# Second parts of the split of two blocks of FFN rows: made on VectorE instead of GpSimd

## The chip, the cores and the metric

One core of one Trainium2 chip runs the kernel. The metric is the device time of one execution in microseconds. The engines are named as the profile names them: PE is TensorE, DVE is VectorE, ACT is ScalarE, POOL is GpSimd, SP is the queue that issues most transfers.

## The reference, cut to what matters

One layer of a decoder for 512 prompt rows and 32 sample rows of width 1024: a mixer, cross-attention to a memory, and a gated feed-forward network (FFN) with a short convolution. The change lies where cross-attention ends and the FFN begins:

```python
x = x + rms_norm(mem_attend(rms_norm(x, g_mem_pre), mk, mv, w_mq, w_mo), g_mem_post)
f, conv_new = conv_ffn(rms_norm(x, g_ffn_pre), conv_buf, w_up, w_dw, b_dw, w_down)
x = x + rms_norm(f, g_ffn_post)
```

`rms_norm` divides each row by the root of its mean square and multiplies by a gain. `conv_ffn` first computes `u = h @ w_up`, with 5504 output columns.

## The kernel before

**Split products.** A float32 operand of a large product is kept as two parts in the format fp32r: a first part, the operand cast to fp32r, and a second part, the operand minus the first. A product is made of three matmuls: first by first, first by second, second by first. `split` makes both parts: the first always on ACT, the second on DVE, or on another engine if one is passed in. Weights are split in the same way after they arrive (tile `wst` into tile `wslot`, 128x1024 each).

**The boundary.** The rows lie in five blocks: blocks 0 to 3 with 128 prompt rows each, block 4 with the 32 sample rows. The last projection of cross-attention (tile `oT` times `w_mo`) goes through its second 512 output columns block by block, in the order 4, 0, 1, 2, 3 (`proj_add`, `second`). For each block `ev1` makes a sum of squares on ACT (`sqj`), a product with the gain on DVE (`y`, L1128), the sum `ssy` on DVE (L1129), the power -1/2 of it on POOL (`rs`, L304), and two additions into the residual rows `xb` on DVE (L1134). `rows_of` then makes the mean square of the new rows on ACT (`sqx`, L309), its power -1/2 on POOL, and a copy `rsd` on DVE, and puts the block on a list.

**Transposed rows.** `norm_turn` takes a block from that list. It transposes its 1024 columns on PE in two quads of four 128x128 tiles each (L328, into the PSUM tile `tp`), multiplies a quad by the gain on DVE (`ht`, L330), and splits it into the tiles of `fT` (first part on ACT, L146, second part L147). In the instruction order below `fT_6086` and `fT_6098` are the first parts of quads 0 and 1, and `fT_6087` and `fT_6099` the second parts. The tuple `pool` says for each quad whether its second part is made on POOL (`True`) or on DVE (`False`). The factor of each row isn't multiplied into `fT`; `spread` broadcasts it with a small matmul over the partitions (tile `rsb` in PSUM, one matmul for each block) and DVE copies it to SBUF (`rsb`, line 1565). The PSUM tiles `tp` and `rsb` share three buffers.

**The first FFN products.** The first four tiles of `u` are computed in two halves of rows (`half_first` in `gemmB`, L465): for columns 0 to 255 of `fT` (blocks 0 and 1) all four tiles, 24 matmuls each, and then for columns 256 to 543 (blocks 2, 3 and 4). Blocks 2 and 3 are transposed between the tiles of the first half (`POS`). All later tiles (L477) take both halves together.

**The order.** A scheduler decides at build time, from its own estimate of times, in which order each engine gets its instructions; each engine then keeps that order. So a change of one instruction's engine can move others.

```python
def split(hi, lo, src, eng=None):
    nc.scalar.copy(out=hi, in_=src)
    (eng or nc.vector).tensor_tensor(out=lo, in0=src, in1=f32(hi), op=SUB)
```

Of the kernel before, what the change touches and what calls it, by code (L numbers as in the profile page):

```python
# [77 lines left out]
def kernel(ctx: ExitStack, tc: tile.TileContext, I, O):  # L78
# [8 lines left out]
    ACTROWS, POOLQ = True, (True, True)  # L87
# [17 lines left out]
    def N(name, w=1024):  # L105
        return npool.tile([P, 1032], F32, name=name, tag="N")[:, :w]

    def T2(shape, name, dt=F32):
        return t2p.tile(list(shape), dt, name=name, tag="T2")

    def Z(name):
        return zp.tile([P, 512], F32, name=name, tag="Z")
# [36 lines left out]
    def rows(b):  # L149
        return (b * P, P) if b < 4 else (SEQ, NS)  # L150
# [147 lines left out]
    def rstd(ss, n, w, dim, name="rs"):  # L298

        r = small(w, name)  # L300
        if dim is not None:
            nc.gpsimd.tensor_scalar(out=r[:n], in0=ss, scalar1=1.0 / dim, scalar2=EPS, op0=MUL, op1=ADD)
            ss = r[:n]
        GTT(out=r[:n], in0=ss, in1=mhalf[:n, :w], op=ALU.pow)  # L304
        return r[:n]

    def sumsq(x, n, junk, name="ssq"):
        ss = small(1, name)
        ACT(out=junk, in_=x, func=AF.Square, accum_out=ss[:n])  # L309
        return ss[:n]  # L310

    def norm_rows(x, n, act=False):
        h = N("hN")[:n]
        rs = rstd(sumsq(x, n, h), n, 1, DM)
        if act:
            nc.scalar.mul(out=h, in_=x, mul=rs)
        else:
            VTS(out=h, in0=x, scalar1=rs, scalar2=None, op0=MUL)
        return h

    def norm_turn(h, n, gname, xt, c0, pool=(True, False)):

        tmps = []
        for q in range(2):
            ps = at("tp")
            pv = v2(ps, P)[:, :, :n]
            for j in range(4):
                tr(pv[:, j, :], h[:, (4 * q + j) * P:(4 * q + j + 1) * P], ident[:n, :n])  # L328
            tmp = T2([P, 4, n], "ht")
            VTT(out=tmp, in0=pv, in1=gcol(gname, 4 * q, 4 * q + 4).unsqueeze(2).broadcast_to([P, 4, n]), op=MUL)  # L330
            put(xt, q, 0, 4, c0, n, tmp, nc.gpsimd if pool[q] else None)
            tmps.append(tmp)
        return tmps
# [15 lines left out]
    class Fill:  # L349
# [8 lines left out]
        def run(self, amount=1e9):  # L358
            while amount > 0 and self.q:
                try:  # L360
                    amount -= next(self.q[0])
                except StopIteration:
                    self.q.pop(0)
# [25 lines left out]
    def sample_sum(ps, dst):  # L389
        for e in range(2):  # L390
            c = slice(256 * e, 256 * e + 256)
            nc.scalar.copy(out=dst[:, c], in_=ps[NS * e:NS * e + NS, :256])
            VTT(out=dst[:, c], in0=ps[64 + NS * e:64 + NS * e + NS, :256], in1=dst[:, c], op=ADD)
# [260 lines left out]
    for c0, c1 in HALF:  # L654
        n = c1 - c0
# [433 lines left out]
    def gbc(name):  # L1089
        g = cst.tile([P, 1028], F32, name="gb", tag="gb")  # L1090
        dma(out=g[:, :DM], in_=I[name][0].partition_broadcast(P))
        return g[:, :DM]

    def proj_add(xt, gname, src, gname2, dst, order=None, scale=None):

        g = gbc(gname)
        y0, s0, xb, pend, ready, target = {}, {}, {}, [], [], []

        def ssq(b, y, nm):
            n = rows(b)[1]  # L1100
            ss = sm.tile([P, 1], F32, name=nm, tag=nm, bufs=6)
            j = Z("sqj")
            ACT(out=j[:n], in_=y, func=AF.Square, scale=DM ** -0.5, accum_out=ss[:n])
            return ss[:n]

        def ev0(b, ps):
            n = rows(b)[1]
            z = y0[b] = T2([P, 512], "y0")[:n]
            if b == 4:
                sample_sum(ps, z)  # L1110
                ps = z
            s0[b] = ssq(b, ps, "ssy0")
            VTT(out=z, in0=ps, in1=g[:n, :512], op=MUL)

        def before(b):
            for c in [4, 0, 1, 2, 3] if scale else [b]:
                if c not in xb:
                    xb[c] = N("xb")[:rows(c)[1]]
                    dma(out=xb[c], in_=src(c))

        def ev1(b, ps):
            c0, n = rows(b)
            z = T2([P, 512], "y1")[:n]
            if b == 4:
                sample_sum(ps, z)
                ps = z
            ss = ssq(b, ps, "ssy1")
            VTT(out=z, in0=ps, in1=g[:n, 512:], op=MUL)  # L1128
            STT(out=ss, in0=s0[b], scalar=EPS, in1=ss, op0=ADD, op1=ADD)  # L1129
            rs = rstd(ss, n, 1, None)  # L1130
            x = xb[b]
            for i, z in enumerate((y0[b], z)):
                c = slice(512 * i, 512 * i + 512)
                STT(out=x[:, c], in0=z, scalar=rs, in1=x[:, c], op0=MUL, op1=ADD)  # L1134
            dma(out=dst[c0:c0 + n, :], in_=x)
            ready.append((x, n, c0))
            while len(ready) > LR:
                rows_of(*ready.pop(0))

        def rows_of(x, n, c0):  # L1140
            if scale is None:
                pend.append((norm_rows(x, n, ACTROWS), n, gname2, target[0], c0, POOLQ))
                return
            pend.append((x, n, gname2, target[0], c0, POOLQ))
            rs = sm.tile([P, 1], F32, name="rsd", tag="rsd", bufs=5)
            VCP(out=rs[:n], in_=rstd(sumsq(x, n, Z("sqx").bitcast(BF16)[:n]), n, 1, DM))
            scale[1].append((rs[:n], c0, n))

        def mid():
            if len(pend) > LP:  # L1150
                norm_turn(*pend.pop(0))

        def second(xt2):
            target.append(xt2)
            run(gemmA(xt, 8, [4, 0, 1, 2, 3], ev1, block_major=True, before=before, mid=mid, midk=1 if scale else MIDK))
            while ready:
                rows_of(*ready.pop(0))
            while len(pend) > 2:
                norm_turn(*pend.pop(0))
            return pend  # L1160
        return gemmA(xt, 8, order or allb, ev0, block_major=order is not None, halves=True), second
# [157 lines left out]
    pend = second(hqT)  # L1319
# [250 lines left out]
    pend = second(fT)  # L1570
# [307 lines left out]
```

## Time and profile before

| What | Value |
|---|---|
| time, median of 3 runs | 960.0 us (959.2 to 962.14) |
| profiled execution: its time, its span | 957.37 us, 955.6 us |
| PE busy in the span | 933.3 us, 98% |
| DVE busy | 600.3 us, 63% |
| ACT busy | 387.7 us, 41% |
| POOL busy | 196.4 us, 21% |
| mean granted clock of PE | 0.994 of full speed |

The span runs from the first to the last instruction of the profiled execution. Busy shares are means over stages with different limits. The boundary between cross-attention and FFN lies between 541 and 576 us of the span. Below, an instruction's row gives its start, its duration, and in brackets how long the engine sat idle ahead of it and what ended that.

### The profile page before, as it was taken

The page shows a single profiled execution, that of the slowest core. Times are in us where ns is not written, and L with a number is a line of the kernel's source. Part 1 is how long each engine was busy: PE and PEld are TensorE (multiplying, and loading weights), DVE is VectorE, ACT ScalarE, POOL GpSimd, SP SyncE. Part 2 cuts the span into 40 slices and gives each one's busy share as a digit, 9 for nine tenths or more (in the row PEclk, how much of TensorE's full clock was granted, in tenths as well). Part 3 has the DMA queues.
Part 4 walks back from the last instruction along what each step waited for, and adds up shares of the span by engine and source line. Part 5 has one row for each costly group of instructions (what it writes and reads, how often), then busy time and mean ns, then how long its engine had stood idle before and what let it go on. Part 6 is the DMA issues. An engine that isn't in the chain of part 4 may idle for free. (4 is left out here: it accounts for less than half of the span.)

```text
span 955.6 us, 17087 instructions
## 1 busy us (share of the span) xinstructions
PE 933.3 (98%) x6619; PEld 810.2 (85%) x6619; DVE 600.3 (63%) x1129; ACT 387.7 (41%) x750; POOL 196.4 (21%) x383
## 2 busy tenths in 40 slices
PE   8999999999999999999999999999999999999995
PEld 5899787889766778998767799989988997999974
DVE  6745145565886448635654769727758676676767
ACT  5655134344676357635544523332212222222232
POOL 6610000115432216300000454001110110110114
PEclk9999999999999999999999999999999999999998
DMA  8950023344825539946954743063053313512023
GB/s 296 296 178 1 1 88 136 88 131 137 275 82 171 173 100 346 289 137 188 344 195 115 206 133 88 4 177 89 4 144 82 119 26 81 162 48 89 24 92 116
DMA packets 120674, 130.27 MB, mean 136 GB/s; under 512 B 8568, under 2 KB 86233, under 8 KB 120593
## 3 DMA queue, kind: packets, MB, share of 16 engines
q1 hardware_dynamic: 114408, 125.69, 42.3%
q10 hardware_dynamic: 6184, 3.48, 1.2%
q8 instruction: 52, 0.85, 0.4%
q14 instruction: 30, 0.24, 0.1%
HBM read 112.22 MB, written 16.93 MB: 135 GB/s over the span
## 5 line engine op out<-in xcount | busy, mean ns | idle before, releaser
L146 ACT CAST wslot<-wst 128x1024 fp32r<-128x1024 f32 x125 | 130.8, 1050 | 261.3 <-issue 73.5
L477 PE MATMUL mm<-fT,wslot 128*128 128x256 f32 x1872 | 235.9, 288 | 0.0
L477 PEld LDWEIGHTS mm<-fT,wslot 128*128 128x128 f32 x1872 | 234.4, 188 | 1.8 <-issue 0.8
L147 DVE TENSOR_TENSOR wslot<-wst,wslot 128x1024 fp32r<-128x1024 f32 x125 | 154.4, 1238 | 91.8 <-ACT wslot L146 91.4
L1689 PE MATMUL mm<-wslot,act 128*128 128x512 f32 (+1 forms) x180 | 70.2, 391 | 0.0
L1690 PE MATMUL mm<-wslot,act 128*128 128x512 f32 (+1 forms) x180 | 70.0, 392 | 0.0
L1688 PE MATMUL mm<-wslot,act 128*128 128x512 f32 (+1 forms) x180 | 69.3, 387 | 0.0
L1596 POOL COPY cvo<-u 128x2 f32<-128x2 f32 x43 | 11.0, 256 | 204.7 <-DVE u L1594 194.6
L407 PE MATMUL mm<-wslot,hT 128*128 128x512 f32 x128 | 51.6, 403 | 0.0
L477 PE MATMUL mm<-hT,wslot 128*128 128x256 f32 (+1 forms) x384 | 51.0, 289 | 0.0
L409 PE MATMUL mm<-wslot,hT 128*128 128x512 f32 x128 | 51.0, 400 | 0.0
L408 PE MATMUL mm<-wslot,hT 128*128 128x512 f32 x128 | 50.7, 396 | 0.0
L1591 DVE TENSOR_TENSOR u<-mm,rsb 128x256 f32<-128x256 f32 x43 | 18.2, 424 | 51.0 <-PE mm L477 50.0
L477 PEld LDWEIGHTS mm<-hT,wslot 128*128 128x128 f32 x384 | 49.2, 188 | 0.5 <-issue 0.2
L1688 PEld LDWEIGHTS mm<-wslot,act 128*128 128x128 f32 x180 | 34.3, 191 | 8.0 <-issue 0.4
L1690 PEld LDWEIGHTS mm<-wslot,act 128*128 128x128 f32 x180 | 33.8, 188 | 7.2 <-issue 0.4
L1689 PEld LDWEIGHTS mm<-wslot,act 128*128 128x128 f32 x180 | 33.8, 188 | 7.2
L1608 ACT ACTIVATE c<-c 128x560 f32<-128x560 f32 x21 | 14.1, 672 | 56.5 <-DVE c L1602 56.5
L1602 DVE SCALAR_TENSOR_TENSOR c<-u,cvT,c 128x560 f32<-128x560 f32 x43 | 34.3, 798 | 0.9
L1601 DVE SCALAR_TENSOR_TENSOR c<-u,cvT,c 128x560 f32<-128x560 f32 x43 | 34.1, 793 | 0.2
L1701 DVE TENSOR_TENSOR yp<-mm,yp 128x512 f32<-128x512 f32 (+1 forms) x41 | 27.2, 674 | 5.1 <-PE mm L1690 5.0
L409 PEld LDWEIGHTS mm<-wslot,hT 128*128 128x128 f32 x128 | 24.1, 188 | 5.1
(474 smaller groups left out, 1863.8 us busy)
## 6 DMA issues: line engine op xcount, KB each, us to landing
wst<-in_w_up_dram SPq DMA_DIRECT2D x42, 512.0 KB
wst<-in_w_in_dram SPq DMA_DIRECT2D x28, 512.0 KB
wst<-in_w_down_dram SPq DMA_DIRECT2D x20, 512.0 KB
wst<-in_cache_mem_k_dram SPq DMA_DIRECT2D x16, 512.0 KB
wst<-in_w_mk_dram SPq DMA_DIRECT2D x8, 512.0 KB
xb<-in_x_prompt_dram SPq DMA_DIRECT2D x8, 512.0 KB
wst<-in_cache_dk_dram SPq DMA_DIRECT2D x16, 256.0 KB
wst<-in_cache_dv_dram SPq DMA_DIRECT2D x16, 256.0 KB
```

The costliest lines, as they stand in the source:

```text
L146: nc.scalar.copy(out=hi, in_=src)
L147: (eng or nc.vector).tensor_tensor(out=lo, in0=src, in1=f32(hi), op=SUB)
L407: mm(ps[b], lhsT=xt.hi(k, c0, c0 + n), rhs=s[:, 0, kk, :], start=(k == 0), stop=False)
L408: mm(ps[b], lhsT=xt.hi(k, c0, c0 + n), rhs=s[:, 1, kk, :], start=False, stop=False)
L409: return mm(ps[b], lhsT=xt.lo(k, c0, c0 + n), rhs=s[:, 0, kk, :], start=False, stop=(k == nk - 1))
L477: mm(ps[i], lhsT=s[:, l, k, :], rhs=x(k, c0, c1), start=(k == 0 and j == 0), stop=(k == 7 and j == 2))
L1601: STT(out=c, in0=u[:, 1:EXT - 1], scalar=w[1], in1=c, op0=MUL, op1=ADD)
L1602: STT(out=c, in0=u[:, 0:EXT - 2], scalar=w[0], in1=c, op0=MUL, op1=ADD)
L1688: mm(ps, lhsT=t[:, 0, c0:c0 + P], rhs=s[:, 0, i % 2, cs], start=st, stop=False)
L1689: mm(ps, lhsT=t[:, 0, c0:c0 + P], rhs=s[:, 1, i % 2, cs], start=False, stop=False)
L1690: return mm(ps, lhsT=t[:, 1, c0:c0 + P], rhs=s[:, 0, i % 2, cs], start=False, stop=en)
L1701: VTT(out=y, in0=ps, in1=y, op=ADD)
```

## The change

For the rows that the FFN reads, blocks whose first row lies below 256 (blocks 0 and 1) go onto the list with `(False, False)` in place of `POOLQ`, which is `(True, True)`. So the second parts of their four quads, 128x512 each, are made on DVE instead of POOL. Blocks 2, 3 and 4 keep POOL, and so do the rows that go into cross-attention.

```diff
             if scale is None:
                 pend.append((norm_rows(x, n, ACTROWS), n, gname2, target[0], c0, POOLQ))
                 return
-            pend.append((x, n, gname2, target[0], c0, POOLQ))
+
+            pend.append((x, n, gname2, target[0], c0, (False, False) if c0 < 256 else POOLQ))
             rs = sm.tile([P, 1], F32, name="rsd", tag="rsd", bufs=5)
             VCP(out=rs[:n], in_=rstd(sumsq(x, n, Z("sqx").bitcast(BF16)[:n]), n, 1, DM))
             scale[1].append((rs[:n], c0, n))
```

The changed kernel has one line more, so lines behind this place count one higher in it (the broadcasts are L1564 before and L1565 now, their copies L1565 and L1566). The order moves on two engines in places that the prediction speaks of.

On DVE, from the multiplication of block 1's quad 0 by the gain to the sum `ssy` of block 3, before:

```order
L330 TENSOR_TENSOR ht<-tp,gT 128x512
L1134 SCALAR_TENSOR_TENSOR xb<-y_5954,rs,xb 128x512
L1134 SCALAR_TENSOR_TENSOR xb<-y_6186,rs,xb 128x512
L147 TENSOR_TENSOR wslot<-wst,wslot 128x1024
L330 TENSOR_TENSOR ht<-tp,gT 128x512
L147 TENSOR_TENSOR wslot<-wst,wslot 128x1024
L1565 COPY rsb<-rsb 128x32
L1565 COPY rsb<-rsb 128x128
L147 TENSOR_TENSOR wslot<-wst,wslot 128x1024
L1128 TENSOR_TENSOR y_6268<-mm,gb 128x512
L1129 SCALAR_TENSOR_TENSOR ssy_6269<-ssy_5960,ssy_6269 128x1
```

The same place in the changed kernel (ahead of these rows stand now block 0's `fT_6087`, both additions into `xb` of block 2 and, as before, one weight split):

```order
L330 TENSOR_TENSOR ht<-tp,gT 128x512
L147 TENSOR_TENSOR fT_6099<-ht,fT_6098 128x4x128
L147 TENSOR_TENSOR wslot<-wst,wslot 128x1024
L330 TENSOR_TENSOR ht<-tp,gT 128x512
L147 TENSOR_TENSOR wslot<-wst,wslot 128x1024
L1566 COPY rsb<-rsb 128x32
L1566 COPY rsb<-rsb 128x128
L1147 COPY rsd<-rs 128x1
L147 TENSOR_TENSOR wslot<-wst,wslot 128x1024
L1128 TENSOR_TENSOR y_6268<-mm,gb 128x512
L1129 SCALAR_TENSOR_TENSOR ssy_6269<-ssy_5960,ssy_6269 128x1
L147 TENSOR_TENSOR fT_6087<-ht,fT_6086 128x4x128
```

Block 0's second part of quad 1 (`fT_6099`) now stands between the two gain products of block 1, and block 1's second part of quad 0 (the last row) stands behind all four weight splits, the copies of `rsb` and block 3's `y` and `ssy`.

On PE, from the end of the projection into the first FFN products, before:

```order
L409 MATMUL mm<-wslot,oT_5661 128x512
L1564 MATMUL rsb<-cpk,rsd 128x32
L1564 MATMUL rsb<-cpk,rsd 128x128
L465 MATMUL mm<-fT_6086,wslot 128x256 x4
L465 MATMUL mm<-fT_6087,wslot 128x256
L465 MATMUL mm<-fT_6086,wslot 128x256 x2
```

Further on before, 28 matmuls of L465 behind the second broadcast, the third broadcast (block 1's row factors), and then block 2's transposes:

```order
L465 MATMUL mm<-fT_6086,wslot 128x256
L1564 MATMUL rsb<-cpk,rsd 128x128
L465 MATMUL mm<-fT_6086,wslot 128x256
L465 MATMUL mm<-fT_6087,wslot 128x256
L465 MATMUL mm<-fT_6086,wslot 128x256 x2
L465 MATMUL mm<-fT_6087,wslot 128x256
L465 MATMUL mm<-fT_6086,wslot 128x256 x2
L465 MATMUL mm<-fT_6087,wslot 128x256
L465 MATMUL mm<-fT_6098,wslot 128x256
L328 MATMUL tp<-cpk,xb 128x128 x8
```

The same place in the changed kernel, from the end of the projection:

```order
L409 MATMUL mm<-wslot,oT_5661 128x512
L1565 MATMUL rsb<-cpk,rsd 128x32
L1565 MATMUL rsb<-cpk,rsd 128x128 x2
L465 MATMUL mm<-fT_6086,wslot 128x256 x4
L328 MATMUL tp<-cpk,xb 128x128 x8
L465 MATMUL mm<-fT_6087,wslot 128x256
```

The third broadcast now stands ahead of the first FFN matmul (the row with x2), and block 2's eight transposes stand behind the first four of these matmuls instead of behind 37. ACT's order moves with it: the first part of block 1's quad 0 stood ahead of the cast of the fourth weight tile, and now stands behind block 2's `sqx`, that cast and block 3's `sqj`.

## Rows read from the trace of the kernel before

**Rows 1.** Timeline of PE: start us, us, instruction, [idle before <-what ended it]
```profile
545.38 0.82 PE L1564 MATMUL rsb<-cpk,rsd 32*128 32x32 f32 x4
546.08 0.74 PE L465 MATMUL mm<-fT,wslot 128*128 128x256 f32 x4
548.09 3.12 PE L465 MATMUL mm<-fT,wslot 128*128 128x256 f32 x24 [1.28 <-POOL fT L147]
551.05 0.38 PE L1564 MATMUL rsb<-cpk,rsd 128*128 128x128 f32 x2
551.19 1.30 PE L465 MATMUL mm<-fT,wslot 128*128 128x256 f32 x9
552.33 1.04 PE L328 MATMUL tp<-cpk,xb 128*128 128x128 f32 x8
553.12 4.52 PE L465 MATMUL mm<-fT,wslot 128*128 128x256 f32 x36
...
561.45 0.77 PE L465 MATMUL mm<-fT,wslot 128*128 128x288 f32 x4
562.72 12.50 PE L465 MATMUL mm<-fT,wslot 128*128 128x288 f32 x92 [0.49 <-POOL fT L147]
```

**Rows 2.** The chain that ended last, in order of time: start us, us, what
```profile
575.22 23.95 PE mm L477 x192
```

**Rows 3.** Timeline of DVE, the same stretch
```profile
541.67 0.69 DVE L1128 TENSOR_TENSOR y<-mm,gb 128x512 f32<-128x512 f32 x1 [0.66 <-ACT sqj L1103]
542.27 1.25 DVE L1129 SCALAR_TENSOR_TENSOR ssy<-ssy,ssy 128x1 f32<-128x1 f32 x1
...
543.51 1.21 DVE L147 TENSOR_TENSOR wslot<-wst,wslot 128x1024 fp32r<-128x1024 f32 x1
544.64 0.68 DVE L330 TENSOR_TENSOR ht<-tp,gT 128x512 f32<-128x512 f32 x1
545.24 3.34 DVE L1134 SCALAR_TENSOR_TENSOR xb<-y,rs,xb 128x512 f32<-128x512 f32 x2
...
551.38 0.38 DVE L1565 COPY rsb<-rsb 128x32 f32<-128x32 f32 x2
...
554.36 0.14 DVE L1129 SCALAR_TENSOR_TENSOR ssy<-ssy,ssy 128x1 f32<-128x1 f32 x1
...
555.15 1.42 DVE L1134 SCALAR_TENSOR_TENSOR xb<-y,rs,xb 128x512 f32<-128x512 f32 x2 [0.39 <-POOL rs L304]
556.49 1.28 DVE L330 TENSOR_TENSOR ht<-tp,gT 128x512 f32<-128x512 f32 x2
```

**Rows 4.** Timeline of POOL, the same stretch
```profile
542.22 1.29 POOL L147 TENSOR_TENSOR fT<-ht,fT 128x512 fp32r<-128x512 f32 x1 [0.26 <-ACT fT L146]
543.60 1.51 POOL L304 TENSOR_TENSOR rs<-ssy,mhalf 128x1 f32<-128x1 f32 x1
545.09 2.95 POOL L147 TENSOR_TENSOR fT<-ht,fT 128x512 fp32r<-128x512 f32 x2
```

**Rows 5.** Timeline of ACT, the same stretch
```profile
543.52 1.99 ACT L146 CAST wslot<-wst 128x1024 fp32r<-128x1024 f32 x2
...
548.68 1.06 ACT L309 ACTIVATE sqx<-xb 128x1024 bf16<-128x1024 f32 x1 [1.70 <-DVE xb L1134]
```

**Rows 6.** DVE groups by form, whole span: xcount | busy us, mean ns
```profile
L1616 DVE TENSOR_TENSOR a<-c 128x512 f32<-128x512 f32 x21 | 14.5, 691 | 13.6 <-ACT c L1608 13.6
...
L147 DVE TENSOR_TENSOR memT<-ht,memT 128x512 fp32r<-128x512 f32 x2 | 2.9, 1438 | 0.0
```

**Rows 7.** Timeline of PE at the start of the program
```profile
8.67 1.94 PE L328 MATMUL tp<-cpk,xm 128*128 128x128 f32 x8 [2.18 <-DVE wslot L223]
```

**Rows 8.** Windows: busy of PE, PEld, DVE, ACT, POOL (x), then PEclk
```profile
8.50:9.00 0.50, 0.33 (x2) 0.36 (x3) 0.07 (x1) 0.00 (x0) 0.50 (x1) 0.50 1.07 397
...
11.00:11.50 0.50, 0.50 (x3) 0.50 (x2) 0.50 (x2) 0.50 (x2) 0.47 (x1) 0.50 1.05 389
...
547.00:548.00 1.00, 0.00 (x0) 0.00 (x0) 1.00 (x1) 0.00 (x0) 1.00 (x1) 1.00 1.08 327
```

## Prediction, made before the changed kernel ran

> **What bounds the kernel now.** I read the table first: PE is busy nearly all of the span, so only what makes PE wait or run slower can move the end. The chain that ended last then shows whether later work has slack: behind the boundary it is PE's own matmuls without a break, from 575.22 us on in stretches such as 24 us of L477 [rows 2]. So a delay of PE at the boundary reaches the end in full, and a gain does too. The next view is PE's timeline across the boundary [rows 1]. The last projection ends about 545.4, two broadcasts of row factors follow, and the FFN starts at 546.08 with four matmuls that need first parts only. Then PE waits 1.28 us for POOL, which is making the second part of block 1's quad 0. From 548.09 to 561 the first half of the rows runs with the transposes of blocks 2 and 3 in between. At 562.72 there is a second wait for POOL, 0.49 us, for block 3. These two waits, 1.77 us, are what the change can win at most as idle time.
>
> DVE's timeline [rows 3] shows why one should be careful with it: from 541.67 to 555 it is hardly ever free, and some of its rows are much longer than their kind. A sum of one column takes 1.25 us where it takes 0.14 alone; a pair of additions takes 3.34 where the next takes 1.42. POOL's timeline [rows 4] has a subtraction of 128x512 beside each of them (542.22 to 543.51, 545.09 to 548.04). The two engines hold each other up: POOL's one-column power at 543.60 takes 1.51, and ends 0.39 after DVE's weight split of 543.51 to 544.72.
>
> **The change, part by part.** Four subtractions of 128x512 leave POOL and go to DVE. On POOL one took 1.29 alone [rows 4]. On DVE the trace has the same shape from SBUF at 0.691 us (L1616, 21 times) and, where POOL was at work beside it, at 1.438 (`memT`, twice) [rows 6]. I take 0.69, because in the changed order POOL has only operations of one to sixteen columns there. Below 0.60 it can't come, half of a weight split's 1.21 [rows 3]. What goes with the four from POOL is the delay that they gave DVE: 1.1 us at the sum and 1.9 at the additions. So DVE does not get more work in all, but the order, not the sum, decides here.
>
> *DVE, step by step*, each step from start to next start [rows 3]: 0.60 for a product with the gain (541.67 to 542.27; the same for `ht`, 544.64 to 545.24), 1.13 for a weight split (543.51 to 544.64), 1.34 for a pair of additions (555.15 to 556.49), 0.07 for a one-column operation, 0.38 for the two copies of `rsb`, and 0.60 for a second part by its likeness to `ht`. Up to 541.67 nothing changes. Block 2's `y`: to 542.27; `ssy` and `rsd`: to 542.41; block 0's first second part: to 543.10, its end. Block 2's additions wait for POOL's power; it is held by that subtraction as the one at 543.60 was, so it ends 0.39 after it, and they start at 543.50. From there DVE has no wait: additions to 544.84, weight split to 545.97, `ht` of block 1's quad 0 to 546.57, second part to 547.17, weight split to 548.30, `ht` of block 1's quad 1, which ends at 548.98, the next from 548.90, weight split to 550.03, copies of `rsb` to 550.41, `rsd` to 550.48, the fourth weight split to 551.61, block 3's `y` and `ssy` to 552.28, and only then block 1's second part of quad 0, done at 552.97. Before, POOL had it done at 548.04 [rows 4].
>
> *PE behind it.* The third broadcast now stands ahead of the first FFN matmul. `tp` and `rsb` share three buffers, so it needs the one that block 1's quad 1 leaves when its `ht` is done: 548.98. Before, that broadcast stood 28 matmuls further on, at 551.05 [rows 1], and stopped nobody. ACT arrives no sooner: after two weight casts that end at 545.51 it now does block 2's sum of squares (1.06 [rows 5]), a weight cast (half of 1.99), block 3's half-width sum of squares and then the first part of block 1's quad 0, some 549. So PE stands from 545.7 to 549.0, with nothing queued ahead to fill it. Then four matmuls; then block 2's transposes, which need both copies of `rsb` (550.4) and last about 1 us; then it waits again until 553.0 for the second part.
>
> *The sum.* At 553.12 PE before had 37 of the first half's 96 matmuls and block 2's transposes behind it [rows 1]. At 553.0 it now has 4 and the same transposes. The missing 33 cost 0.122 each (36 from 553.12 to the transposes that follow, 24 from 548.09 to 551.05 in 2.96): 4.0 us. Less the 0.1 that it starts earlier. Less the second wait: four matmuls of the second half take 0.54 at 12.50 / 92, so the next could have come at 561.99 and came at 562.72, a loss of 0.73. It goes now, since PE is late and POOL is not: PE has block 3's transposes behind it at about 562.3, its second part follows by 564.6 (two steps of 0.6 and 1.29 on POOL), and PE asks for it at about 565.9. 4.0 - 0.1 - 0.7 = **+3.2 us**. DVE's other work, ACT and the queues stay ahead of PE as before, since the next weights wait for slots that PE frees; if that cover fell away, the steps behind would grow by the same delay, not more.
>
> Both ends of the unknown costs: three of the subtractions lie ahead of the step that PE waits for, so at 1.44 each the delay is 3 x 0.75 = 2.2 more, +5.4; at 0.60 and without POOL's held-up power (0.39) it is 0.3 + 0.4 less, +2.5.
>
> The profiled execution took 957.37 us, 2.6 less than the median 960.0; the step is the same for both. 957.4 + 3.2 = 960.6 for such an execution, and **963.2 us** as a median.
>
> **Rivals.**
>
> *The clock falls as well: +4.6, 964.6.* The granted clock is at its upper level, 2.4 GHz, through the boundary, also in the microsecond of 547 to 548 in which PE did nothing [rows 8]. At the program's start PE did eight transposes, stood 2.18 us, and resumed at 0.50, which is 1.2 GHz; the same eight transposes that take 1.04 [rows 1] took 1.94 [rows 7], and the level was still 0.50 up to 11.5 [rows 8]. So some 3 us of matmuls at the lower level cost 3 x (1 - 1.04 / 1.94) = 1.4 us. For it: PE now stands 3.3 us, then works about 1.5, then stands 1.8. Against it: it isn't idle in one piece, and no stretch of this trace has just this pattern. The Trainium skill ("TensorE: Matmul & The Clock Gate", section on HAM oscillation) says that gaps between bursts of matmuls bring the lower clock back; rows 7 and 8 agree for the start of the program, and rows 1 and 8 show a gap of 1.28 us that did not do it.
>
> *The waits only change places: +1 to +2.4, about 961.7.* This needs DVE to reach block 1's second part 0.8 to 2 us sooner than I add up. For it: with POOL quiet, weight splits or additions could be a little shorter than any row here. Against: the rows I took the steps from are among the shortest of their kind.
>
> *Faster: -1.8, 958.2.* If the second part of block 1 were there when PE asks at 546.8, both waits for POOL would be gone and nothing else lost. The place is that wait; the point from which it decides is whether `ht` of block 1's quad 1 is done by 545.5 and the second part by 546.6. For it: 0.69 on DVE against 1.29 on POOL. Against: `ht` isn't due until 548.9, because two second parts, a pair of additions and two weight splits stand ahead of it on DVE. The Trainium skill ("GPSIMD Engine Reference", 4.1 Engine selection) puts elementwise work on VectorE and calls GpSimd about twice as slow with two inputs. Rows 4 and 6 agree (1.29 against 0.69), and by that rule alone the time would be this rival's; the order is what it leaves out.
>
> *DVE is slowed as at the program's start: +5.4, 965.4.* The upper end above; against it, POOL's large subtractions are gone from that stretch.
>
> **How the numbers follow.** A measurement of this kernel can tell 0.3%, 2.9 us, from no change. Chances: the forecast 0.45; with the clock 0.28; waits that change places 0.15; faster 0.07; DVE slowed 0.05. The forecast's own spread, +2.5 to +4, has the 2.9 inside; I give 0.27 of its 0.45 to above. Slower: 0.27 + 0.28 + 0.05 = 0.60. Faster by over 0.3%: not even the whole 1.8 reaches it, 0.03. No change: 0.37. The range goes from +1, which takes in most of the waits that change places, to +5.4: 961.0 to 965.4; it leaves out the faster case and some of the edges, less than 0.2.
>
> **What would show it.** Right: in PE's timeline the broadcasts run in two pieces with the second at about 549, the first four FFN matmuls follow it, block 2's transposes come ahead of the first second part, and that comes at about 553 released by DVE; the first half ends near 565 and L477 starts near 578.3 instead of 575.1; no wait for POOL at block 3. On DVE, `ssy` takes 0.14 and the additions 1.4. In the windows, a granted clock below 1.00 between 548 and 558 would speak for the clock rival. Wrong: the second part of block 1 done well before 552, a third broadcast that didn't wait for `ht`, or a delay at the boundary that is gone by the end.

## The result and the profile after

The changed kernel took 962.62 us (median of 20 executions, 960.22 to 967.89) against 958.84 for the kernel before (20 executions, 956.24 to 963.07): a ratio of 1.0038, 95% interval 1.0026 to 1.005, so +3.8 us by the medians. It is slower; whether by more than 0.3% the interval leaves open. The prediction was 963.2 us, and +3.2.

PE's timeline of the changed kernel, over the stretch of [rows 1] (start us, us, instruction, [idle before <-what ended it]):

```profile
544.90 0.40 PE L409 MATMUL mm<-wslot,oT 128*128 128x512 f32 x1
545.23 0.40 PE L1565 MATMUL rsb<-cpk,rsd 32*128 32x32 f32 x2
546.67 0.49 PE L1565 MATMUL rsb<-cpk,rsd 128*128 128x128 f32 x2 [1.04 <-DVE ht L330]
549.00 0.80 PE L1565 MATMUL rsb<-cpk,rsd 128*128 128x128 f32 x2 [1.84 <-DVE ht L330]
549.45 1.20 PE L465 MATMUL mm<-fT,wslot 128*128 128x256 f32 x4
550.45 1.91 PE L328 MATMUL tp<-cpk,xb 128*128 128x128 f32 x8
552.89 10.67 PE L465 MATMUL mm<-fT,wslot 128*128 128x256 f32 x69 [0.53 <-DVE fT L147]
563.39 1.04 PE L328 MATMUL tp<-cpk,xb 128*128 128x128 f32 x8
...
567.36 13.01 PE L465 MATMUL mm<-fT,wslot 128*128 128x288 f32 x96
580.21 19.98 PE L477 MATMUL mm<-fT,wslot 128*128 128x256 f32 x159
```

The third broadcast waits for `ht` until 549.00, four FFN matmuls and block 2's transposes follow, and PE resumes at 552.89, when DVE has made block 1's second part. From there on the second wait of before (0.49 for block 3) is gone: the second half's 96 matmuls run from 567.36 in one piece of 13.01, and the later tiles (L477) start at 580.21 where they started at 575.06. From the third broadcast on, rows take longer than their like in [rows 1]: four matmuls 1.20 in place of 0.74, eight transposes 1.91 in place of 1.04, and the 69 matmuls, from start to next start, 0.152 each in place of 0.122.

DVE's timeline, over the stretch of [rows 3]:

```profile
542.21 0.15 DVE L1129 SCALAR_TENSOR_TENSOR ssy<-ssy,ssy 128x1 f32<-128x1 f32 x1
...
542.34 0.68 DVE L147 TENSOR_TENSOR fT<-ht,fT 128x512 fp32r<-128x512 f32 x1
543.46 1.42 DVE L1134 SCALAR_TENSOR_TENSOR xb<-y,rs,xb 128x512 f32<-128x512 f32 x2 [0.43 <-POOL rs L304]
...
546.53 0.68 DVE L147 TENSOR_TENSOR fT<-ht,fT 128x512 fp32r<-128x512 f32 x1
...
548.26 0.68 DVE L330 TENSOR_TENSOR ht<-tp,gT 128x512 f32<-128x512 f32 x1
548.86 1.22 DVE L147 TENSOR_TENSOR wslot<-wst,wslot 128x1024 fp32r<-128x1024 f32 x1
549.99 0.38 DVE L1566 COPY rsb<-rsb 128x32 f32<-128x32 f32 x2
...
550.35 1.21 DVE L147 TENSOR_TENSOR wslot<-wst,wslot 128x1024 fp32r<-128x1024 f32 x1
551.48 0.68 DVE L1128 TENSOR_TENSOR y<-mm,gb 128x512 f32<-128x512 f32 x1
...
552.15 1.29 DVE L147 TENSOR_TENSOR fT<-ht,fT 128x512 fp32r<-128x512 f32 x2
```

Step by step it is the chain of the prediction: second part of block 0 at 542.34, additions at 543.46 behind POOL's power, `ht` of block 1's quad 1 at 548.26 to 548.94, and the last row, in which two second parts stand together, from 552.15. The sum `ssy` takes 0.15 and the additions 1.42, as the shorter rows of their kind in [rows 3].

Windows of the changed kernel (start:end, length, busy of PE, PEld, DVE, ACT, POOL with counts, then the granted clock, the DMA share and GB/s):

```profile
547.00:547.50 0.50, 0.15 (x2) 0.00 (x0) 0.50 (x2) 0.50 (x2) 0.50 (x1) 1.00 0.53 146
547.50:548.00 0.50, 0.00 (x0) 0.00 (x0) 0.50 (x1) 0.50 (x3) 0.50 (x1) 0.62 0.68 193
548.00:549.00 1.00, 0.00 (x1) 0.00 (x1) 1.00 (x3) 0.54 (x3) 0.92 (x3) 0.50 1.10 333
...
553.00:557.50 4.50, 4.50 (x21) 4.50 (x22) 4.18 (x6) 1.42 (x3) 3.72 (x7) 0.50 0.83 306
557.50:558.00 0.50, 0.50 (x5) 0.50 (x4) 0.00 (x0) 0.50 (x1) 0.50 (x1) 0.64 0.00 0
```

PE's clock falls to 0.50 (1.2 GHz) while PE stands for `ht` the second time, and is back at 1.00 (2.4 GHz) only at about 558. This execution's mean clock was 0.989 of full speed, where the profiled one of before had 0.994. The 20 executions fall into two groups by that figure: 14 at 0.988 to 0.991, mean 963.5 us, and 6 at 0.993 to 0.995, mean 961.0. So the lower clock came in most executions, not in all. The figure is a mean over the whole span; only a profiled execution shows where the clock fell.

### The profile page after: what moved, and what is told of

The parts are those of the page before. It is cut to its first block, busy times and chain, and to the rows that moved or that the text cites. A ratio compares the mean times of both kernels' runs of the same rounds, so it can differ in the third digit from the quotient of the medians.

```text
span 960.4 us, 17088 instructions
## 1 busy us (share of the span) xinstructions
PE 937.0 (98%) x6619; PEld 813.8 (85%) x6619; DVE 598.4 (62%) x1133; ACT 388.0 (40%) x750; POOL 191.6 (20%) x379
## 5 line engine op out<-in xcount | busy, mean ns | idle before, releaser
L477 PE MATMUL mm<-fT,wslot 128*128 128x256 f32 x1872 | 235.9, 288 | 0.0
L477 PEld LDWEIGHTS mm<-fT,wslot 128*128 128x128 f32 x1872 | 234.4, 188 | 1.8 <-issue 0.8
L477 PE MATMUL mm<-hT,wslot 128*128 128x256 f32 (+1 forms) x384 | 51.0, 289 | 0.0
L477 PEld LDWEIGHTS mm<-hT,wslot 128*128 128x128 f32 x384 | 49.2, 188 | 0.5 <-issue 0.2
```

What stands on the lines that cost most here:

```text
L477: mm(ps[i], lhsT=s[:, l, k, :], rhs=x(k, c0, c1), start=(k == 0 and j == 0), stop=(k == 7 and j == 2))
```

## The experiments

Two theories stood against each other. **The order**: what costs time is where block 1's `ht` and second part stand in DVE's queue, behind weight splits, and what PE does until they come; the lower clock is added where PE stands long. **The rival**: four subtractions moved to a busy engine cost their time there, each its share of 3.8 us. To compare traces I measure the boundary from the start of the last projection matmul to the first row of the later tiles, less the 2.6 us of 22 matmuls of later tiles where a kernel does these earlier: 30.0 us in the profiled execution of before, and 35.3 after the change. Before_again is the kernel before once more; its trace gives 29.6, so two traces of one kernel differ here by 0.4.

| Kernel | Ratio to before, 95% | us by the ratio | Boundary, us | Executions at 0.991 or less |
|---|---|---|---|---|
| changed | 1.0038 (1.0026 to 1.0050) | +3.6 | 35.3 | 14 of 20 |
| first_quads | 1.0064 (1.0049 to 1.0079) | +6.1 | 35.5 | 4 of 6 |
| second_quads | 0.9998 (0.9989 to 1.0007) | -0.2 | 28.7 | 1 of 12 |
| block0_only | 1.0025 (1.0013 to 1.0037) | +2.4 | 33.5 | 4 of 10 |
| block1_only | 1.0036 (1.0025 to 1.0046) | +3.5 | 33.9 | 7 of 12 |
| broadcast_late | 1.0063 (1.0046 to 1.0079) | +6.0 | 36.4 | 4 of 6 |
| splits_late | 1.0000 (0.9989 to 1.0011) | 0.0 | 30.3 | 1 of 12 |
| both_late | 0.9999 (0.9987 to 1.0010) | -0.1 | 28.9 | 0 of 12 |
| both_late_again | 0.9981 (0.9972 to 0.9990) | -1.8 | 29.2 | 1 of 11 |
| keep_busy | 1.0033 (1.0021 to 1.0045) | +3.2 | 33.1 | 1 of 8 |
| fill_first | 1.0035 (1.0022 to 1.0048) | +3.4 | 32.8 | 1 of 7 |
| fill_second | 1.0032 (1.0019 to 1.0045) | +3.1 | 33.6 | 2 of 11 |
| before_again | 0.9996 (0.9984 to 1.0007) | -0.4 | 29.6 | 1 of 12 |

**One half of the change at a time.** Only the tuple or the condition in the change's line differs; the four added lines are, in this order, those of first_quads, second_quads, block0_only and block1_only:

```diff
-            pend.append((x, n, gname2, target[0], c0, (False, False) if c0 < 256 else POOLQ))
+            pend.append((x, n, gname2, target[0], c0, (False, True) if c0 < 256 else POOLQ))
+            pend.append((x, n, gname2, target[0], c0, (True, False) if c0 < 256 else POOLQ))
+            pend.append((x, n, gname2, target[0], c0, (False, False) if c0 == 0 else POOLQ))
+            pend.append((x, n, gname2, target[0], c0, (False, False) if c0 == 128 else POOLQ))
```

first_quads:

> Only the second parts of quad 0 of blocks 0 and 1 go to DVE; those of quad 1 stay on POOL. Theory of the order: DVE still makes block 1's quad 0 behind all four weight splits, and PE still has the third broadcast ahead of the FFN, so PE resumes only about 0.6 us sooner than in the changed kernel (one subtraction less ahead of it), near 552.3: +2.5 to +3.5 us against before. Rival, each subtraction moved to DVE simply costs its share: two of four, half of 3.8, so +1.9 us.

second_quads:

> Only the second parts of quad 1 of blocks 0 and 1 go to DVE; those of quad 0 stay on POOL, and PE's order stays that of before (third broadcast behind some 27 FFN matmuls). Theory of the order: POOL makes block 1's quad 0 one subtraction (1.3 us) earlier in its queue, but its first part ends only at 546.0, so the second is there at 547.3 in place of 548.04: -0.5 us against before (-0.8 to 0), and no third broadcast that waits. Rival, each subtraction moved costs its share: +1.9 us.

The two halves measured +6.1 and -0.2 us: not 1.9 each, so the rival falls. For first_quads the order theory had the sign but not the size: +2.5 to +3.5 was expected. Part of the reason is in its trace. DVE's timeline:

```profile
542.93 2.46 DVE L1134 SCALAR_TENSOR_TENSOR xb<-y,rs,xb 128x512 f32<-128x512 f32 x2 [0.43 <-POOL rs L304]
...
550.28 1.93 DVE L147 TENSOR_TENSOR wslot<-wst,wslot 128x1024 fp32r<-128x1024 f32 x1
...
553.00 0.69 DVE L147 TENSOR_TENSOR fT<-ht,fT 128x512 fp32r<-128x512 f32 x1
```

POOL's, the same stretch:

```profile
543.11 1.74 POOL L147 TENSOR_TENSOR fT<-ht,fT 128x512 fp32r<-128x512 f32 x1 [0.21 <-ACT fT L146]
...
549.59 1.53 POOL L147 TENSOR_TENSOR fT<-ht,fT 128x512 fp32r<-128x512 f32 x1 [1.27 <-ACT fT L146]
```

And PE, where it resumes:

```profile
553.74 9.80 PE L465 MATMUL mm<-fT,wslot 128*128 128x256 f32 x69 [1.62 <-DVE fT L147]
```

POOL's two subtractions lie beside the additions and the fourth weight split and lengthen them by 1.0 and 0.7 us, more than the 0.6 that the shorter queue saves; block 1's second part starts at 553.00, 8.4 us behind the start of the last projection matmul (544.64 here), against 7.3 in the changed kernel, and PE resumes 1.1 us later than there. In this profiled execution the lower clock ended sooner, so the 69 matmuls took 9.80 in place of 10.67, and the boundary is only 0.2 longer than the changed kernel's. That first_quads is slower than the changed kernel rests on the times, six executions whose interval just touches that of the changed kernel. In second_quads the part that PE waits for is POOL's and the queue order is that of before:

```profile
545.51 0.72 PE L465 MATMUL mm<-fT,wslot 128*128 128x256 f32 x4
547.15 3.71 PE L465 MATMUL mm<-fT,wslot 128*128 128x256 f32 x29 [0.92 <-POOL fT L147]
```

PE's one wait is 0.92 here, and none comes at block 3, where PE now has 22 matmuls of later tiles ahead of it. The gain at this boundary is 1.3 us against the first trace of before and 0.9 against before_again's; the time doesn't show it, its interval goes from -1.1 to +0.7 us.

block0_only:

> Only block 0's second parts go to DVE, block 1's stay on POOL. PE's order is that of the changed kernel (third broadcast ahead of the FFN), but POOL makes block 1's second part of quad 0 as soon as its first part is there, near 550. Theory of the order: PE resumes when block 2's transposes end, near 551.4 in place of 552.9, so +1.5 us against before at the upper clock, up to +3.5 where the clock falls. Rival, each subtraction costs its share: +1.9 us in every execution. The trace tells them apart: by the theory PE does not wait for a second part at all.

block1_only:

> Only block 1's second parts go to DVE, block 0's stay on POOL. In this order four FFN matmuls stand ahead of the third broadcast, and block 1's second part of quad 0 stands behind three weight splits and a copy of rsb on DVE, near 551.3. Theory of the order: PE resumes there with 92 matmuls and half of block 2's transposes left, where before had 92, the transposes and a broadcast at 548.09: +3.2, less 0.5, 0.2 and 0.7 for block 3, +1.8 us, up to +4 in executions in which the clock falls. Rival, each subtraction costs its share: +1.9 us in all; the two differ in the trace, where by the theory PE has one wait of about 3 us for DVE's second part, and by the rival none longer than before.

block0_only came out at +2.4 us, inside what was expected, and its trace has no wait of PE for a second part: it waits 1.18 and 1.85 for `ht`, ahead of the second and the third broadcast, and runs on from there:

```profile
548.83 0.49 PE L1565 MATMUL rsb<-cpk,rsd 128*128 128x128 f32 x2 [1.18 <-DVE ht L330]
551.16 0.79 PE L1565 MATMUL rsb<-cpk,rsd 128*128 128x128 f32 x2 [1.85 <-DVE ht L330]
```

So with block 1's parts back on POOL the stands ahead of the early broadcasts are what is left of the loss, about two thirds by the times. block1_only (+3.5, inside what was expected) was to have one wait for DVE's second part; the trace has the long wait elsewhere:

```profile
546.59 0.74 PE L465 MATMUL mm<-fT,wslot 128*128 128x256 f32 x4
549.89 0.80 PE L1565 MATMUL rsb<-cpk,rsd 128*128 128x128 f32 x2 [2.56 <-DVE ht L330]
551.12 1.12 PE L328 MATMUL tp<-cpk,xb 128*128 128x128 f32 x4 [0.44 <-DVE rsb L1566]
551.89 4.40 PE L465 MATMUL mm<-fT,wslot 128*128 128x256 f32 x19
```

It is again the third broadcast that stands for `ht`, and this one stand of 2.56 is followed by the lower clock:

```profile
550.00:551.00 1.00, 0.69 (x2) 0.39 (x2) 1.00 (x3) 0.49 (x1) 1.00 (x3) 0.50 0.62 152
```

Blocks 0 and 1 cost 2.4 and 3.5 alone, and 3.6 together: shares don't add up, since they are one delay of PE.

**The order put back, the work left on DVE.** In broadcast_late the third broadcast is tied behind the last of tile 0's 24 matmuls; in splits_late the second parts of the four weight tiles are tied behind block 1's second part of quad 0; both_late has both.

```diff
-            mm(ps[:, :n], lhsT=rs.broadcast_to([n, P]), rhs=ident[:n, :n], start=True, stop=True)
+            with tc.issue_after(seen[0]) if c0 == 128 else ExitStack():
+                mm(ps[:, :n], lhsT=rs.broadcast_to([n, P]), rhs=ident[:n, :n], start=True, stop=True)
```

Here `seen[0]` is the last of those 24 matmuls; below, `lo` is the subtraction behind which the splits go:

```diff
+            lo = los.get(("fT", 0, 128))
+            if lo is not None and len(held) < 4:
+                held.append(1)
+                nc.scalar.copy(out=sv[:, 0], in_=st)
+                with tc.issue_after(lo.ins):
+                    nc.vector.tensor_tensor(out=sv[:, 1], in0=st, in1=f32(sv[:, 0]), op=SUB)
+                return
```

broadcast_late:

> The changed kernel with one thing put back: the third broadcast is queued behind tile 0's 24 FFN matmuls again, block 2's transposes behind it. DVE's order stays that of the changed kernel. Theory that the place of block 1's second part of quad 0 on DVE (behind four weight splits) decides: PE does four matmuls from about 548.5, stands until 552.9 as before this edit, and then has block 2's transposes still to do (1.04), so +4 us against before at the upper clock and up to +6.5 where the clock falls. Rival, the third broadcast's wait is the cause: putting it back takes the loss away, 0 to +1 us.

splits_late:

> The changed kernel with another thing put right: on DVE the four weight splits are queued behind block 1's second part of quad 0; all four second parts stay on DVE, and the third broadcast stays ahead of the FFN. Theory of the order: ht of block 1's quad 1 is done near 546.6 in place of 548.9, the third broadcast, block 2's transposes and the second part follow by 548.3, and PE then has 96 matmuls left where before had 92, the transposes and a broadcast at 548.09: -1.3 us against before with no wait at block 3, or -0.4 if the first FFN tile is one of the four whose split is now late (1.2 us). Rival, four subtractions on DVE cost their time wherever they stand: +3 to +4 us.

both_late, and the same kernel a second time:

> Both edits on the changed kernel: weight splits behind block 1's second part of quad 0, and the third broadcast behind tile 0. Theory of the order: the second part is there near 547.6 (548.8 if the first tile's split is late), against 548.04 before, and PE's order is that of before: -0.7 to +0.7 us. Rival, the subtractions cost their time on DVE: +3 to +4 us.

> The kernel with both edits once more, for a narrower figure. Its trace has the boundary 1.1 us shorter than before's (from the last projection matmul to the first matmul of the later tiles, without the 22 of these that it does earlier). If nothing is given back later, the time is 0.5 to 1.2 us below before's; if later work takes it back, it is the same as before within 0.1%.

PE in broadcast_late (the projection's last matmul starts at 546.60 here):

```profile
550.15 1.22 PE L467 MATMUL mm<-fT,wslot 128*128 128x256 f32 x4 [1.43 <-ACT fT L146]
554.46 6.29 PE L467 MATMUL mm<-fT,wslot 128*128 128x256 f32 x31 [3.09 <-DVE fT L147]
```

With the broadcast out of the way PE stands for the second part instead, 3.09 us, until the same point of DVE's queue (7.9 us behind that matmul, 8.0 in the changed kernel), and has block 2's transposes still ahead of it: +6.0, inside the +4 to +6.5 that was expected. The broadcast's place by itself is not what to mend. DVE in splits_late:

```profile
546.31 0.68 DVE L341 TENSOR_TENSOR ht<-tp,gT 128x512 f32<-128x512 f32 x1
...
547.78 0.68 DVE L147 TENSOR_TENSOR fT<-ht,fT 128x512 fp32r<-128x512 f32 x1
548.38 2.36 DVE L225 TENSOR_TENSOR wslot<-wst,wslot 128x1024 fp32r<-128x1024 f32 x2
```

And PE:

```profile
547.05 0.49 PE L1576 MATMUL rsb<-cpk,rsd 128*128 128x128 f32 x2 [0.45 <-DVE ht L341]
547.37 1.04 PE L339 MATMUL tp<-cpk,xb 128*128 128x128 f32 x8
548.16 6.39 PE L476 MATMUL mm<-fT,wslot 128*128 128x256 f32 x52
555.59 4.18 PE L476 MATMUL mm<-fT,wslot 128*128 128x256 f32 x33 [1.03 <-DVE fT L147]
```

All four second parts are still on DVE, and the loss is gone: ratio 1.0000, interval 0.9989 to 1.0011. (The scheduler also moved block 2's transposes ahead of the first FFN matmul here.) PE waits 0.45 for `ht` and starts the FFN at 548.16 without a stop for block 1. What I had not forecast is the wait of 1.03 at 555.59, for a second part of quad 1 that now stands behind the four splits; it eats the gain of 1.3 that one of the two cases had. In both_late PE has one wait, 0.61 for ACT, and no other at the boundary:

```profile
546.17 8.16 PE L478 MATMUL mm<-fT,wslot 128*128 128x256 f32 x63 [0.61 <-ACT fT L146]
```

Its time was 0.5 us below before by the means of the first run (12 executions against 27) and 1.9 in the second (11 against 15). The second is more than the 0.5 to 1.2 that was expected, and its interval excludes no change; the first's includes it. The traces say 1.1 and 0.8 against the first trace of before, 0.7 and 0.5 against before_again's. Some 0.7 of this is before's loss at block 3, where 22 matmuls of later tiles now stand. It is clearly faster than the changed kernel, and probably faster than before by up to about 1 us, but two runs that differ by so much don't settle that.

**The clock.** keep_busy puts small bf16 matmuls of zeros into PE's queue, 16 ahead of the broadcasts and 14 behind the third; fill_first has only the 16, fill_second only the 14. The zeros land in a PSUM tile that the next product starts anew.

```diff
+                    if xt.name == "fT" and i == 0 and ev in evacs[:2]:
+                        with tc.issue_after(seen[2]) if seen else ExitStack():
+                            for _ in range(14 if seen else 16):
+                                mm(ps, lhsT=warm[:, 0:P], rhs=warm[:, 0:c1 - c0], start=True, stop=True)
```

keep_busy:

> The changed kernel with 16 small bf16 matmuls of zeros on PE between the projection and the broadcasts, and 14 between the third broadcast and the first FFN matmul; their results are overwritten. They fill PE's two waits and nothing waits for them. If the lower clock of 548 to 558 comes from the waits and costs 2.1 us in the executions that have it, the granted clock stays at 1.00 here and the time is about +2 us against before (960.9), with 0.994 or 0.995 as mean clock in nearly all executions. If the clock isn't set by the waits, or costs nothing, +3.8 as in the changed kernel. PE resumes at 552.9 in either case.

before_again:

> The kernel before, unchanged, to see the mean granted clock of each of its executions. If the lower clock at the boundary comes with the change, all executions of before have about 0.994; if executions of before lose it just as often, they show 0.989 to 0.991 too, and the clock explains none of the difference. Time: the same as before, within 0.15%.

fill_first and fill_second:

> The changed kernel with the first filler alone: 16 small matmuls of zeros between the projection and the broadcasts, nothing in the second wait. If the wait ahead of the third broadcast is what brings the lower clock, most executions keep 0.993 or more here, and the time is that with both fillers, +3.0 us against before. If the second wait (for block 1's second part) does it alone, the clock falls as in the changed kernel (0.988 to 0.991 in two of three executions), and the time is +3.8 to +4.1.

> The changed kernel with the second filler alone: 14 small matmuls of zeros behind the first FFN matmul, so the wait ahead of the third broadcast stays empty. If that first wait brings the lower clock, it falls as in the changed kernel, 0.988 to 0.991 in most executions, at +3.8 to +4.5 us (the fillers run at the lower clock too); if the second does it alone, 0.993 or more and +3.0.

PE in keep_busy (last projection matmul at 546.41):

```profile
546.65 1.92 PE L468 MATMUL mm<-warm 128*128 128x256 bf16 x16
...
550.56 0.49 PE L1571 MATMUL rsb<-cpk,rsd 128*128 128x128 f32 x2 [1.23 <-DVE ht L330]
550.88 1.69 PE L468 MATMUL mm<-warm 128*128 128x256 bf16 x14
...
554.45 8.46 PE L471 MATMUL mm<-fT,wslot 128*128 128x256 f32 x69 [0.37 <-DVE fT L147]
```

The window of its longest stand that is left:

```profile
549.00:551.00 2.00, 0.77 (x6) 0.55 (x7) 2.00 (x3) 1.55 (x4) 1.49 (x3) 1.00 0.84 249
```

PE resumes 8.0 us behind the start of the last projection matmul, as in the changed kernel: the order's delay is all there. But the clock stays at 1.00, and the same 69 matmuls take 8.46 in place of 10.67. The boundary is 33.1 us, 3.1 above before (3.5 above before_again): this is the order alone, and the time says the same, +3.2. I had expected about +2; by the ratios the fillers gave back 0.4 of +3.6, and medians over executions with and without the fall don't settle why it isn't more. The lower clock is 2.2 us of the changed kernel's profiled 5.3, by the same rows.

That the fall comes with PE's standing shows in the counts of executions. Of 101 executions of before that ran beside these kernels or as before_again, 8 had a mean clock of 0.991 or less; of 26 with a filler, 4; of the changed kernel's 20, 14. My expectation that all executions of before would have 0.994 was too simple, they go from 0.990 to 0.997. Between the two waits the fillers did not decide: either one made the low figure rare. In fill_second's profiled execution the clock did fall as the empty first wait ended (549.54), but was back before the 69 matmuls:

```profile
549.50:553.00 3.50, 3.46 (x16) 2.63 (x17) 3.50 (x8) 0.62 (x1) 0.14 (x1) 0.51 0.89 191
553.00:555.00 2.00, 2.00 (x19) 1.99 (x18) 1.77 (x4) 0.00 (x0) 2.00 (x5) 1.00 1.01 387
```

So fillers have a price too. These 14 took 3.00 at 1.2 GHz where keep_busy's took 1.69, mostly while PE had nothing else to do; the 69 matmuls start 8.5 us behind the last projection matmul, 0.4 later than in keep_busy. By the median the clock's share in the changed kernel is small: the filled kernels' ratios (1.0032 to 1.0035) lie inside the interval of 1.0038. What shows it are the trace's 2.2 us and the 2.5 between the two groups of executions, not the ratios.

## Why the prediction was right, point by point

*DVE's chain.* Right to about 0.1 us: `ht` of block 1's quad 1 was to end at 548.98 and ended at 548.94; the second part was to end at 552.97, and PE resumed at 552.89. Most of what the sum was late by is the two copies of `rsb`, counted with their duration of 0.38 where the next instruction started 0.30 after them. The price of a second part, 0.69 from [rows 6], came as 0.68; the delays that go away with POOL's subtractions went (0.15 for `ssy`, 1.42 for the additions).

*PE behind it.* Right: third broadcast at 549.0, four matmuls, transposes, a wait for DVE, no wait at block 3. The first stand came in two pieces, since the second broadcast waits for `ht` too (1.04), which delays nothing here. The later marks, the first half's end near 565 and L477 near 578.3, came some 2 us late (567.0 and 580.21); that is the clock.

*The sum.* +3.2 was the order's price, and with the fillers the order alone measured +3.1 to +3.4. The six executions of the changed kernel that kept 0.993 or more, without fillers, put it lower: their mean of 961.0 is 2.2 above before's median. In the profiled execution: 4.0 for the 33 missing matmuls, less 0.2 for the earlier resume, less 0.7 for block 3, plus 2.2 for the clock is 5.3, and the later tiles start 5.15 later. It reaches the end nearly in full: that execution took 4.85 longer than the profiled one of before (962.22 and 957.37).

*The clock.* This is the term that was mis-sized, twice. I put it as a rival of 0.28 against a forecast without it; it was a share of executions, 14 of 20. And it cost 2.2 in the trace, not 1.4, since the lower level lasted to about 557.9, 5.0 us into the 69 matmuls, not the 3 us that I took from the program's start [rows 8]. The Trainium skill ("TensorE: Matmul & The Clock Gate", section on HAM oscillation) describes bursts of matmuls with waits between them that bring the lower clock back; the changed kernel's windows agree, with stands of 1.04 and 1.84 us and 0.49 of work between them, and [rows 1, 8] show a single one of 1.28 that did not; block1_only's single one of 2.56 did.

*The base.* The 960.0 was a median of three; over 20 executions before is 958.84. So the time's nearness is in part luck: 1.2 too much in the base and 0.6 too little in the step (the clock, left out of it, is the term that fits) leave 963.2 for 962.62, 0.6 off with the other sign.

*The other rivals.* The waits did not change places by a sooner DVE, and nothing was faster. DVE slowed by POOL did not happen ahead of the step that PE waits for. Behind it it did, where POOL makes block 2's second parts (additions of 2.43 at 554.75), and PE didn't stand for that; first_quads shows it ahead of that step.

## What to carry to other kernels

Moving work to an engine that does it in half the time says nothing until you have read what stands ahead of it in that engine's queue: here 0.68 us for 1.29 was bought with a place behind four weight splits, and PE paid some 3 us for it; with the same work in a better order the loss was gone. When such a move reorders two engines, undo each order by itself before you blame the work: putting back the visible one (the broadcast) only moved the wait. And where a change makes TensorE stand longer or several times in a row, count the clock after the waits as a cost that comes in some executions: look at each execution's granted clock, not at the median alone.

## What the runs showed of the hardware

In these rows DVE and POOL hold each other up for whole instructions where both work out of SBUF, and not where DVE reads PSUM. Beside a POOL subtraction a pair of additions took 2.46 (first_quads) and 3.34 [rows 3] in place of 1.42, and a weight split 1.93 for 1.21; POOL's copy of 16 columns took 1.13 for 0.19 beside DVE's split in the changed kernel:

```profile
549.00 1.13 POOL L1591 COPY u<-cvT 128x16 f32<-128x16 f32 x1
...
554.00 0.19 POOL L1591 COPY u<-cvT 128x16 f32<-128x16 f32 x1
```

`ht`, which multiplies a PSUM tile, took its 0.68 also beside POOL's power [rows 3, 4]. The Trainium skill ("SBUF — State Buffer", section on who interferes with whom) says that the two share a pair of ports that one instruction holds to its end; the rows agree. What I had not expected is that half of a move can be dearer than all of it: with two subtractions left on POOL, DVE's additions and fourth split took 1.8 us more than with none there, and of the two that it was spared (1.4) only one lies ahead of the step that PE waits for.
